# A running-maximum kernel: three engines' programs wrapped in a loop of two rounds, and Pool's products taken two rows at a time

## The chip, the cores and the metric

One core of one Trainium2 chip. The metric is the time of one execution on the device in microseconds, the median of several; a profile of one execution lies beside it. All runs told here were in the same, fast state. A ratio is the mean time of one kernel's fast runs over the mean time of the other's fast runs of the same rounds, so it isn't quite the ratio of the medians quoted. The experiments ran on three chips, each with the kernel before beside them.

## The reference

```python
# x: 8 x 2048 x 4096 float32 (268 MB), w: 4096 x 1
proj = (x @ w).squeeze(-1)                   # 8 x 2048 dot products of length 4096
cm = np.maximum.accumulate(proj, axis=1)
return np.cumsum((proj >= cm).astype(np.float32), axis=1)   # number of records so far
```

Every element of x is used once, so the time can't be below that of reading 268 MB.

## The kernel before

SyncE issues all loads of x. A tile is 128 partitions of 4 (later 3) rows of 4,096; three buffers of 8 MB take turns. Each row is split: VectorE makes the dot product of columns 0 to 2,815 in one instruction, Pool multiplies columns 2,816 to 4,095 and ACT sums that product. TensorE turns the sums so that VectorE can scan them. Eight tiles make a group; groups 0 to 2 are a loop on each engine, the rest is straight code.

```python
V, A, G, T, SY = nc.vector, nc.scalar, nc.gpsimd, nc.tensor, nc.sync
...
for g in range(NG):                        # NG = 4, rows per tile RS = (4, 4, 4, 3)
    r = RS[g]
    for t in range(B):                     # B = 8 tiles in a group, 3 buffers
        i = SY.dma_start(out=at(g, t)[:, : r * D], in_=x[B - 1 - t, ...]).then_inc(xs[t], 16)
        u, n = user_before(g, t)           # who had the buffer
        if n:
            i._wait_ge(*(free(u, n)))
        if g == t == 0:
            A.dma_start(out=w_row, in_=...).then_inc(ws, 16)
...
def group_products(r, g=0):                # Pool
    for t in range(B):
        for j in range(r):
            xl = at(g, t)[:, j * D + VC : (j + 1) * D]
            i = G.tensor_mul(out=xl, in0=xl, in1=w_sb).then_inc(pl, 1)
            if j == 0:
                i._wait_ge(xs[t], 16)

def group_sums(r, g=0):                    # ACT
    for t in range(B):
        for j in range(r):
            i = add_up(at(g, t)[...], sum_p[...])._wait_ge(pl, j + 1)
        i.then_inc(fr[t], 1)               # the buffer is free once VectorE and ACT have said so
        A.sem_inc(pl, -r)
    A.wait_ge(pd, 1).then_inc(pd, -1)

with A.Fori(0, NL):                        # NL = 3; VectorE, Pool and TensorE likewise
    group_sums(R)
group_sums(RS[-1], NL)
... # 128 more rows of each batch entry in ever smaller pieces, then the output
```

Of the kernel before, what the change touches and what calls it, by code (L numbers as in the profile page):

```python
# [2 lines left out]

os.environ.setdefault("NEURON_RT_ULTRASERVER_MODE", "4")

# [8 lines left out]
ACTF = mybir.ActivationFunctionType  # L15
NEG = -3.0e38
LOW = -3.2e38


@with_exitstack  # L20
def kernel(
# [15 lines left out]
    nc = tc.nc  # L37
    P = 128
    B, S, D = x.shape
# [3 lines left out]
    R = RS[0]  # L43
# [7 lines left out]
    VC = 2816  # L51
    PC = D - VC
# [15 lines left out]
    def rows_of(m):  # L68
        return m * H % B, m * H // B * Q
# [9 lines left out]
    def sb(shape, name, **kw):  # L79
        return pool.tile(shape, FP32, name=name, **kw)  # L80
# [6 lines left out]
    w_sb = sb([P, PC], "w_sb")  # L87
# [23 lines left out]
    def sem(name):  # L111
        return tc.alloc_semaphore(f"{name}_{next(ns)}")
# [3 lines left out]
    ws, bw, wc, cs, od, oe, psr, pd, pl, sd, pa, con, fo, ms, p7, mg, pg, ml = (  # L116
        sem(n) for n in "ws bw wc cs od oe psr pd pl sd pa con fo ms p7 mg pg ml".split()
    )
# [1 line left out]
    xq = [(ws, 32), (bw, NW + 16), (wc, 3 + 16), (con, 7 + 16), (fo, 1 + 16)]  # L120
    xq += [(s, 32) for s in xs[:5]] + [(s, 2 * NG + 16) for s in fr[:3]]

    V, A, G, T, SY = nc.vector, nc.scalar, nc.gpsimd, nc.tensor, nc.sync

    def dot(xsl, wsl, dst, seed=0.0):
        return V.tensor_tensor_reduce(  # L126
# [4 lines left out]
    def add_up(xsl, dst):  # L131
        return A.activation(out=xsl, in_=xsl, func=ACTF.Copy, accum_out=dst)  # L132
# [19 lines left out]
    def at(g, t):  # L152
        return xbuf[(t if g < NL else t + NS - 1) % NS]

    def user_before(g, t):
        if t >= NS:
            return t - NS, g + 1
        if g == NL:
            return B - NS + t, g
        return max(u for u in range(B) if u % NS == t), g  # L160

    def free(u, n):
        return (p7, n) if u == B - 1 else (fr[u], 2 * n)

    with tc.tile_critical(no_gpsimd_drain=True):

        for g in range(NG):
            r = RS[g]
            for t in range(B):
                i = SY.dma_start(  # L170
                    out=at(g, t)[:, : r * D],
                    in_=x[B - 1 - t, STARTS[g] : STARTS[g] + r * P, :].rearrange(
                        "(p r) d -> p (r d)", r=r
                    ),
                ).then_inc(xs[t], 16)
                u, n = user_before(g, t)
                if n:
                    i._wait_ge(*(free(u, n)))
                if g == t == 0:
                    A.dma_start(  # L180
                        out=w_row, in_=w.rearrange("(k c) one -> k (c one)", k=NW)
                    ).then_inc(ws, 16)
                if t == 4 and g:
                    SY.dma_start(
                        out=out[:, STARTS[g - 1] : STARTS[g]], in_=cnt
                    )._wait_ge(cs, g + 1).then_inc(od, 16)
# [9 lines left out]
        for i, (m, c0, c1, _, _) in enumerate(TILES):  # L196
            u, xb = slot(m)
            d = SY.dma_start(  # L198
                out=xb[:, c0:c1],
                in_=x[  # L200
                    rows_of(m)[0] : rows_of(m)[0] + H,
                    S0 + rows_of(m)[1] : S0 + rows_of(m)[1] + Q, c0:c1,
                ].rearrange("b i d -> i b d"),
            ).then_inc(xq[i][0], 16)
# [7 lines left out]
            out=identity, in_=identity, compare_op=ALU.not_equal, fill=1.0,  # L212
# [10 lines left out]
        for n, k in enumerate(order):  # L223
            c = k * WC
            dst = w_v[:, c : c + WC] if c < CV else ps
            i = T.matmul(  # L226
                out=dst, lhsT=identity[:NW, k : k + 1].to_broadcast([NW, P]),
                rhs=w_row, start=True, stop=True,
            ).then_inc(bw, 1)
# [11 lines left out]
            out=by_b, in_=identity.rearrange("p (i b) -> p b i", b=H),  # L241
# [3 lines left out]
            out=by_i, in_=identity.rearrange("p (i b) -> p i b", b=H), op=ALU.add,  # L245
            axis=mybir.AxisListType.X,
        ).then_inc(fo, 1)
        V.memset(ps[:B, :N], LOW)._wait_ge(wc, 3).then_inc(psr, 1)  # L248

# [4 lines left out]
        def group_dots(r, g=0):  # L254
            for t in range(B):
                b, xb = B - 1 - t, at(g, t)
                for j in range(r):
                    i = dot(
                        xb[:, j * D : j * D + VC], w_v[:, :VC],
                        sum_v[:, j * B + b : j * B + b + 1],  # L260
                    )
                    if j == 0:
                        i._wait_ge(xs[t], 16)
                i.then_inc(fr[t], 1)
# [6 lines left out]
        V.sem_inc(psr, -3)  # L271
        group_dots(RS[-1], NL)

        def group_products(r, g=0):
            for t in range(B):
                for j in range(r):
                    xl = at(g, t)[:, j * D + VC : (j + 1) * D]
                    i = G.tensor_mul(out=xl, in0=xl, in1=w_sb).then_inc(pl, 1)  # L278
                    if j == 0:
                        i._wait_ge(xs[t], 16)  # L280

        G.wait_ge(wc, 3)
        with G.Fori(0, NL):
            group_products(R)
            G.wait_ge(pg, 1).then_inc(pg, -1)
        group_products(RS[-1], NL)

        def group_sums(r, g=0):
            for t in range(B):
                b = B - 1 - t  # L290
                for j in range(r):
                    i = add_up(
                        at(g, t)[:, j * D + VC : (j + 1) * D],
                        sum_p[:, j * B + b : j * B + b + 1],
                    )._wait_ge(pl, j + 1)
                i.then_inc(fr[t], 1)
                A.sem_inc(pl, -r)
            A.wait_ge(pd, 1).then_inc(pd, -1)

        with A.Fori(0, NL):  # L300
            group_sums(R)
        group_sums(RS[-1], NL)

        def group_rows(r):
# [67 lines left out]
        for m in range(B - 2):  # L372
            k = m // 2
            v, p = acc_v[:, m : m + 1], acc_p[:, m : m + 1]
# [16 lines left out]
        for i in range(B - 2, len(TILES)):  # L391
            n = i - (B - 2)
            m, p = TILES[i][0], TILES[i][4]
# [21 lines left out]
        for a, b, n in ((STARTS[-1], S0, 1), (S0, S, 4)):  # L415
            SY.dma_start(
                out=out[:, a:b], in_=cnt[:, a - STARTS[-1] : b - STARTS[-1]]
            )._wait_ge(cs, NG + n).then_inc(oe, 16)
        G.wait_ge(oe, 32).then_inc(ml, 1)


# [28 lines left out]
```

## Time and profile before

| | before |
|---|---|
| time, median of 3 | 629.82 us (629.65 to 629.83) |
| busy: VectorE, Pool, ACT | 65%, 59%, 29% of the span |
| x read | 268.4 MB in 5,760 packets (queue q1 counts 6,560: 40 more of the output, 760 of 4 bytes) |
| the same, while the stream runs | 434.4 GB/s |
| instruction fetches in the span | 3 packets of 8 KB |

The prediction below shows the lines and reads them. A word on the views: the page lists the DMA queues by number (q1 carries x and the output, q10 the load of w, q14 instructions). In the timeline a row gives start, duration, engine, line of code, operation and, in brackets, the idle time before it and what ended it. The trace holds each DMA packet's start and duration as well; where the text speaks of packets, that is what it reads. A "straggler" is one of the 16 DMA engines whose packets of a tile end clearly after those of the others. The "spread" is the time from the first to the last of the 16 ends.

### The profile page before, as it was taken

How to read it: one execution, taken by the hardware profiler on the slowest of the kernel's cores; microseconds unless marked ns; L12 is line 12 of the kernel's file. 1: busy time of each engine (PE TensorE's matmuls, PEld its weight loads, DVE VectorE, ACT ScalarE, POOL GpSimd, SP SyncE). 2: the span in 40 equal slices, each digit the busy share in tenths (PEclk: the TensorE clock that was granted, in tenths of full speed). 3: DMA queues.
4: the chain of work that ended last, by engine and by line, in shares of the span. 5: the costliest groups of instructions: out<-in, count | busy, mean ns of one | idle time of the engine just before them, and what ended most of it. 6: DMA issues, size and time to landing. Idle time of an engine off the chain costs nothing. (4 is left out here: it accounts for less than half of the span.)

```text
span 627.8 us, 1141 instructions
## 1 busy us (share of the span) xinstructions
PE 29.4 (5%) x96; PEld 13.6 (2%) x96; DVE 407.2 (65%) x294; ACT 181.1 (29%) x274; POOL 370.5 (59%) x149
## 2 busy tenths in 40 slices
PE   8000000000020000000001000000002000000110
PEld 3000000000010000000000000000001000000000
DVE  0755676456776557755578655676556976655797
ACT  1222332123322233222233222332223333232244
POOL 0554676456765557745567555676557666655775
PEclk9999999999999999999996555555555555555565
DMA  9999999999999999999999999999999999999996
GB/s 402 401 468 401 468 401 464 406 463 405 463 405 463 405 463 405 465 405 463 405 463 405 463 405 459 409 460 409 459 420 423 436 442 420 443 442 410 430 429 261
DMA packets 6579, 268.55 MB, mean 428 GB/s; under 512 B 768, under 2 KB 1040, under 8 KB 1584
## 3 DMA queue, kind: packets, MB, share of 16 engines
q1 hardware_dynamic: 6560, 268.50, 98.9%
q14 instruction: 3, 0.02, 0.0%
q10 hardware_dynamic: 16, 0.02, 0.0%
HBM read 268.45 MB, written 0.07 MB: 428 GB/s over the span
## 5 line engine op out<-in xcount | busy, mean ns | idle before, releaser
L126 DVE CUSTOM_DVE_ANT_0 xall<-xall,w_v 128x2816 f32<-128x2816 f32 (+1 forms) x129 | 385.5, 3041 | 180.5 <-DMA xall<-in_x_dram 180.5
L278 POOL TENSOR_TENSOR xall<-xall,w_sb 128x1280 f32<-128x1280 f32 x120 | 344.8, 2905 | 245.9 <-DMA xall<-in_x_dram 242.6
L132 ACT ACTIVATE xall<-xall 128x1280 f32<-128x1280 f32 (+2 forms) x130 | 162.9, 1253 | 427.7 <-POOL xall L278 407.2
L314 PE MATMUL ps<-identity,small 128*8 128x128 f32 x60 | 13.4, 415 | 567.2 <-PEq L311 567.2
L132 ACT ACTIVATION_READ_ACCUMULATOR xall<-xall 128x1 f32 x130 | 24.2, 186 | 0.0
L338 POOL TENSOR_TENSOR xall<-xall,w_sb 128x1280 f32<-128x1280 f32 (+2 forms) x8 | 21.0, 2628 | 3.1 <-DMA xall<-in_x_dram 3.0
L314 PEld LDWEIGHTS ps<-identity,small 128*8 128x8 f32 x60 | 7.5, 128 | 574.3 <-issue 570.2
L142 DVE TENSOR_TENSOR_SCAN cm<-ps,cm,small 8x512 f32<-8x512 f32 (+3 forms) x8 | 7.0, 869 | 19.2 <-PE ps L314 18.8
L226 PE MATMUL w_v<-w,identity 8*128 8x512 f32 x14 | 12.2, 1056 | 0.0
L126 DVE DVE_READ_ACCUMULATOR2_ANT small<- 128x1 f32 x133 | 10.8, 81 | 0.0
L248 DVE MEMSET ps<- 8x512 f32 x1 | 0.5, 485 | 15.7 <-ACT w L237 15.7
L148 DVE TENSOR_TENSOR_SCAN cnt<-ps,cnt,small 8x512 f32<-8x512 f32 (+3 forms) x8 | 7.0, 871 | 0.3
L226 PEld LDWEIGHTS w_v<-w,identity 8*128 8x128 f32 x14 | 4.6, 332 | 7.3 <-issue 7.3
L234 ACT COPY w_sb<-w_v 128x768 f32<-128x768 f32 x1 | 0.8, 798 | 11.4 <-PE w_v L226 11.4
L145 DVE TENSOR_TENSOR ps<-ps,cm 8x512 f32<-8x512 f32 (+3 forms) x8 | 3.9, 486 | 0.3
L349 POOL TENSOR_TENSOR masked<-fold,small 128x4 f32<-128x4 f32 x8 | 1.6, 200 | 3.2 <-DVE small L126 3.2
L126 DVE CUSTOM_DVE_ANT_0 xall<-xall,w_v,small 128x480 f32<-128x480 f32 (+2 forms) x4 | 3.1, 810 | 0.2 <-DVE small L126 0.2
L359 PE MATMUL ps<-fold,masked 128*8 128x32 f32 x20 | 2.0, 234 | 25.3 <-ACT masked L354 17.7
L354 ACT ACTIVATE masked<-fold,small 128x4 f32<-128x4 f32 x10 | 3.0, 298 | 0.3
L338 POOL TENSOR_TENSOR xall<-xall,w 128x640 f32<-128x640 f32 (+1 forms) x2 | 2.3, 1136 | 0.1
L226 PE MATMUL ps<-w,identity 8*128 8x512 f32 x2 | 2.1, 1136 | 2.6 <-DMA w<-in_w_dram 2.6
L233 ACT ACT_TABLE_LOAD x1 | 1.3, 1283 | 2.7 <-DVE fold L244 2.7
(18 smaller groups left out, 5.3 us busy)
## 6 DMA issues: line engine op xcount, KB each, us to landing
xall<-in_x_dram SPq DMA_DIRECT2D x8, 6144.0 KB, 33.5
xall<-in_x_dram SPq DMA_DIRECT2D x6, 2048.0 KB, 42.6
xall<-in_x_dram SPq DMA_DIRECT2D x1, 1264.0 KB, 36.6
xall<-in_x_dram SPq DMA_DIRECT2D x1, 816.0 KB, 39.3
xall<-in_x_dram SPq DMA_DIRECT2D x1, 784.0 KB, 37.9
xall<-in_x_dram SPq DMA_DIRECT2D x2, 240.0 KB, 26.6
xall<-in_x_dram SPq DMA_DIRECT2D x1, 416.0 KB, 39.4
xall<-in_x_dram SPq DMA_DIRECT2D x24, 45.0
```

The costliest lines, as they stand in the source:

```text
L126: return V.tensor_tensor_reduce(out=xsl, in0=xsl, in1=wsl, scale=1.0, scalar=seed, op0=ALU.mult, op1=ALU.add, accum_out=dst,)
L132: return A.activation(out=xsl, in_=xsl, func=ACTF.Copy, accum_out=dst)
L142: V.tensor_tensor_scan(out=cm_, data0=src, data1=low, initial=cm0, op0=ALU.max, op1=ALU.max,)._wait_ge(psr, base).then_inc(psr, 1)
L145: V.tensor_tensor(out=src, in0=src, in1=cm_, op=ALU.is_ge)._wait_ge(psr, base + 1).then_inc(psr, 1)
L148: V.tensor_tensor_scan(out=cnt_, data0=src, data1=low, initial=cnt0, op0=ALU.add, op1=ALU.max,)._wait_ge(psr, base + 2).then_inc(cs, 1)
L226: i = T.matmul(out=dst, lhsT=identity[:NW, k : k + 1].to_broadcast([NW, P]), rhs=w_row, start=True, stop=True,).then_inc(bw, 1)
L278: i = G.tensor_mul(out=xl, in0=xl, in1=w_sb).then_inc(pl, 1)
L314: i = T.matmul(out=ps[:B, j : r * P : r], lhsT=l[:, j * B : (j + 1) * B], rhs=identity, start=k == 0, stop=k == 1,)
L338: G.tensor_mul(out=xl, in0=xl, in1=w_pool(*p))._wait_ge(*xq[i]).then_inc(pl, 1)
L349: return eng.tensor_tensor(out=e, in0=by_b, in1=acc.to_broadcast([P, H]), op=ALU.mult)
L354: return A.activation(out=e, in_=by_b, func=ACTF.Copy, scale=acc)._wait_ge(pa, na).then_inc(ms, 1)
L359: return T.matmul(out=ps[:B, k * Q : (k + 1) * Q], lhsT=masked[:, n * B : (n + 1) * B], rhs=by_i, start=start, stop=stop,)
```

## The change

Python objects record the three engines' programs and emit them later, inside `Fori(0, 2)` with an `If` on the counter. In round 0 the counter is zero, so each engine jumps over its whole program to its end and back again; round 1 runs it. The intent, as far as the code shows it: to touch the later blocks of the program at the very start, so that the instruction fetches don't fall into the stream of x. Besides, Pool takes two of four rows, or three of three, in one instruction, with w read through a zero stride.

```diff
-    V, A, G, T, SY = nc.vector, nc.scalar, nc.gpsimd, nc.tensor, nc.sync
+    V, A, G = Later(), Later(), Later()        # they record; issue() emits
+    T, SY = nc.tensor, nc.sync
...
-                    A.dma_start(
+                    nc.scalar.dma_start(
                         out=w_row, in_=...
...
+        w_one = w_sb.rearrange("p (o c) -> p o c", o=1)
+        def parts(r, t):
+            if r == R:
+                return [(0, R // 2), (R // 2, R)]
+            return [(j, j + 1) for j in range(r)] if t == B - 1 else [(0, r)]
...
-                for j in range(r):
-                    xl = at(g, t)[:, j * D + VC : (j + 1) * D]
-                    i = G.tensor_mul(out=xl, in0=xl, in1=w_sb).then_inc(pl, 1)
+                rows = at(g, t)[:, : r * D].rearrange("p (r d) -> p r d", r=r)
+                for j, k in parts(r, t):
+                    xl = rows[:, j:k, VC:]
+                    i = G.tensor_mul(
+                        out=xl, in0=xl, in1=w_one.to_broadcast([P, k - j, PC])
+                    ).then_inc(pl, 1)
...                                             # ACT waits at the first row of each part
+        for engine, program in ((nc.vector, V), (nc.scalar, A), (nc.gpsimd, G)):
+            with engine.Fori(0, 2) as i:
+                with engine.If(i):
+                    program.issue(engine)
```

More of the change, by code (lines that the diff above doesn't have):

```diff
@@ L2 @@
 import os
-from contextlib import ExitStack
+from contextlib import ExitStack, contextmanager
 os.environ.setdefault("NEURON_RT_ULTRASERVER_MODE", "4")
@@ L17, with __init__, __getattr__, note @@
 LOW = -3.2e38
+class Later:
+    def __init__(self):
+        self.todo = []
+    def __getattr__(self, name):
+        def note(*args, **kw):
+            step = Step(name, args, kw)
+            self.todo.append(step)
+            return step
+        return note
+    @contextmanager
+    def Fori(self, a, b):
+        outer, self.todo = self.todo, []
+        yield
+        outer.append((a, b, self.todo))
+        self.todo = outer
+    def issue(self, engine, todo=None):
+        for step in self.todo if todo is None else todo:
+            if isinstance(step, tuple):
+                a, b, inner = step
+                with engine.Fori(a, b):
+                    self.issue(engine, inner)
+            else:
+                step.issue(engine)
+class Step:
+    def __init__(self, name, args, kw):
+        self.calls = [(name, args, kw)]
+    def _wait_ge(self, *args):
+        self.calls.append(("_wait_ge", args, {}))
+        return self
+    def then_inc(self, *args):
+        self.calls.append(("then_inc", args, {}))
+        return self
+    def issue(self, engine):
+        for name, args, kw in self.calls:
+            engine = getattr(engine, name)(*args, **kw)
 @with_exitstack
@@ L290, in group_sums @@
                 b = B - 1 - t
+                begin = [j for j, _ in parts(r, t)]
                 for j in range(r):
@@ L294, in group_sums @@
                         sum_p[:, j * B + b : j * B + b + 1],
-                    )._wait_ge(pl, j + 1)
+                    )
+                    if j in begin:
+                        i._wait_ge(pl, begin.index(j) + 1)
                 i.then_inc(fr[t], 1)
-                A.sem_inc(pl, -r)
+                A.sem_inc(pl, -len(begin))
             A.wait_ge(pd, 1).then_inc(pd, -1)
@@ L418 @@
             )._wait_ge(cs, NG + n).then_inc(oe, 16)
-        G.wait_ge(oe, 32).then_inc(ml, 1)
+        for engine, program in ((nc.vector, V), (nc.scalar, A), (nc.gpsimd, G)):
+            with engine.Fori(0, 2) as i:
+                with engine.If(i):
+                    program.issue(engine)
+        nc.gpsimd.wait_ge(oe, 32).then_inc(ml, 1)
 _INS = ['x', 'w']
```

## The prediction

> **What bounds the kernel now.** I read the page first (shares, the 40 slices, the queues), then the chain that ended last, then the Pool timeline as a clock for landings, then the queue table cut into ever smaller windows, and at last the packets themselves.
>
> ```profile
> span 627.8 us, 1141 instructions
> PE 29.4 (5%) x96; PEld 13.6 (2%) x96; DVE 407.2 (65%) x294; ACT 181.1 (29%) x274; POOL 370.5 (59%) x149
> DMA  9999999999999999999999999999999999999996
> q1 hardware_dynamic: 6560, 268.50, 98.9%
> q14 instruction: 3, 0.02, 0.0%
> ```
>
> No compute engine is busy for more than two thirds, while the DMA engines are full in 39 of 40 slices. x alone is 268.4 MB. So the stream of x sets the time, and the rest is the start before it and the tail behind it. The chain that ended last says the same:
>
> ```profile
> 498.67 27.27 DMA xall<-in_x_dram
> 525.93 0.07 issue
> 526.00 8.64 POOL xall L278 x3
> ...
> 580.85 39.27 DMA xall<-in_x_dram
> 620.12 0.07 issue
> 620.19 1.76 POOL xall L338
> ```
>
> The reader should look at the two DMA pieces. A three-row tile occupies the stream for 14.5 us (the landings below), yet from issue to landing it takes 27.27 us: the load stood about 12.8 us in the queue behind others. The last one took 39.27 us for a few MB. So when an engine frees a buffer some microseconds earlier or later, only the queueing changes, not the landing. Behind the last landing lie 627.8 - 620.1 = 7.7 us: 5.3 us of sums, turns and scans, then the output's transfer and the closing barrier.
>
> The stream as seen by Pool, which starts on a tile as soon as it lands:
>
> ```profile
> 22.88 11.49 POOL L278 TENSOR_TENSOR xall<-xall,w_sb 128x1280 f32<-128x1280 f32 x4 [20.88 <-DMA xall<-in_x_dram]
> 42.17 11.48 POOL L278 TENSOR_TENSOR xall<-xall,w_sb 128x1280 f32<-128x1280 f32 x4 [7.80 <-DMA xall<-in_x_dram]
> 100.21 11.51 POOL L278 TENSOR_TENSOR xall<-xall,w_sb 128x1280 f32<-128x1280 f32 x4 [7.83 <-DMA xall<-in_x_dram]
> 120.22 11.49 POOL L278 TENSOR_TENSOR xall<-xall,w_sb 128x1280 f32<-128x1280 f32 x4 [8.50 <-DMA xall<-in_x_dram]
> 139.52 11.49 POOL L278 TENSOR_TENSOR xall<-xall,w_sb 128x1280 f32<-128x1280 f32 x4 [7.81 <-DMA xall<-in_x_dram]
> ```
>
> Tiles land every 19.30 us (139.52 - 120.22), except one: 120.22 - 100.21 = 20.01, which is 0.7 us more, and the idle time before it grows from 7.83 to 8.50. The lost time never comes back. The queue table of 95 to 125 us shows what is special there:
>
> ```profile
> q1 hardware_dynamic: 224, 12.58, 97.0%
> q14 instruction: 2, 0.02, 0.1%
> ```
>
> Two of the three instruction fetches of the whole run fall into that tile. Packet by packet: each of 16 DMA engines moves a 64 KB packet of x in 2.418 us, one straight after the other. At 104.362 and 116.460 us a fetch of 8,192 bytes takes 0.309 us on one of them and the x packet behind it takes 2.955 and 2.662 us, so those DMA engines fall 0.84 and 0.55 us behind. A tile has landed when the slowest has finished its eight packets. At the end of tile 4 the 16 ends span 0.50 us; at the end of tile 5 they span 1.07, with two stragglers (119.43 and 119.69 where the other fourteen lie in 118.62 to 119.13), and they stay stragglers, since no DMA engine ever idles. The third fetch, at 486.64, costs its DMA engine 0.53 us, but that one was early enough not to become the slowest.
>
> Who fetches? By 104 us VectorE had run 46 instructions, by 113.5 us ACT 55; at 486 us Pool had just left its loop, some 64 instructions into its program with the loop counted once. Three programs at a similar depth[...]. That these are VectorE, ACT and Pool is an inference, and they are the three that the change wraps.
>
> [...]
> [...]the back edges of the loops at about 171 and 326 us show no fetch at all.
> [...]the fetch at 104.362 starts where an x packet of its DMA engine ends (104.366), and the next x packet starts with the fetch's end.
> [...]One tile is 8.389 MB in 19.31 us = 434.4 GB/s[...].[...]
> [...]
>
> **The change part by part.**
> *The loop of two rounds.* Round 0 tests a register that is zero and branches over the whole program to its end; round 1 runs it. [...] Its effect, and I think its purpose, is that the jump enters the later blocks of code at about 1 us, before x saturates the DMA engines (first load issued at 0.97, first x packet at 2.00 us). The fetches then happen at the start and the stream runs undisturbed. If nothing remains at 104 and 116 us, the spread stays near 0.50 instead of 1.07, and every later landing, the last included, comes 1.07 - 0.50 = 0.57 us earlier. If the fetch still arrives just as the first x packets start, about 1 us after the branch, part of that is lost: an x packet waits up to 0.31 us on three DMA engines. But those are not necessarily the latest ones (the first x packets start anywhere from 2.00 to 2.53). I take 0.40 of the 0.57.
>
> *The later start of three engines.* Pool's identity matrix feeds the weights' broadcast on TensorE (2.6 to 16.6 us), ACT's copies (to 18.1) and VectorE's first scans (to 22.1); the first tile lands at 22.8. A start later by 0.5 us hides; one of 4 us[...] makes VectorE start on tile 0 some 3 us late. But VectorE needs 12.1 us of each 19.3 and Pool 11.5, and the first buffer is needed again only when tile 2 has landed near 61.5 us. Cost: 0. The load of w is issued ahead of the loop and isn't delayed.
>
> *Pool two rows at a time.* Durations by size: 2.905 us for 1,280 columns, 0.730 for 256, hence 2.12 ns per column and 0.19 us per instruction. Two rows: 2,560 x 2.12 + 190 = 5.62 us, where two took 5.74 back to back. A four-row tile: 11.2 instead of 11.5 us. Pool needs 30 fewer instructions of program (32 to 16 in the loop, 24 to 10 behind it). ACT gets its rows in pairs: its last sum ends about 11.2 + 2 x 1.4 = 14.0 us after landing instead of 12.9, and in a three-row tile (one instruction of three rows) 8.3 + 3 x 1.4 = 12.5 instead of 10.0. Buffers come free 1.1 to 2.5 us later against 12.8 us of queue ahead of the stream: 0 on the path. In each group's last three-row tile rows stay single, so the end of the group keeps its latency.
>
> *The tail.* The same instructions in the same order. The loop's exit (add, compare) comes after each engine's last instruction and under the output's transfer, 625.4 to 626.7: 0.
>
> Sum: -0.40 + 0 + 0 + 0, so 629.82 - 0.40 = 629.4 us.
>
> **The rivals.**
> (a) The fetches only move: the first round's fetches meet the first x packets and leave the same DMA engines as far behind as before; or the jump brings more fetches[...]. For it: the 1 us between a load's issue and its first packet is about the time a fetch needs too, so it is a close race. Against: at 2 us a fetch can still be ahead of the x packet. It would give 629.8, or with one more fetch on the slowest DMA engine 629.8 + 0.55 = 630.4.
> (b) A new wait: Pool's larger pieces, or the repeated reading of w through a zero stride, are slower than the durations say, so that buffers come late. Pool would have to go from 11.5 to over 19 us per tile, or a buffer to come 12 us later. Nothing in before speaks for a factor like that; even a rise by half would hide. If it did happen, 5% and more would be lost.
> (c) Nothing of it matters, since the tail is bound by compute: VectorE runs without idle time from 613.2 to 624.1 us. But it starts that run on a landing (0.89 us of waiting before it), so landings that all move by half a microsecond move it too. Otherwise 629.8.
>
> **Range and chances.** The point is the undisturbed stream at 70% of its 0.57. Below it lies the full gain and some scatter (three runs before differ by 0.18), so low 628.9; above it lies rival (a) with an extra fetch, so high 630.4. A change of 2% is 12.6 us. The whole time outside the stream is about 10 us, so faster by 2% can't be; slower would need rival (b). Faster 0.005, same 0.985, slower 0.01.
>
> **What would show each step.** In the profile after: the instruction queue has no packet between 10 and 620 us, but some at the start; Pool's tile 5 comes 19.3 and not 20.0 us behind tile 4; landings from tile 5 on come about half a microsecond earlier, and the last near 619.6; the chain still ends through the last DMA landing; a Pool instruction of 128x2560 takes about 5.6 us, one of 128x3840 about 8.3; Pool waits for each tile's landing as before; ACT waits longer for its first rows. The prediction is wrong if fetches still lie in the stream, if the first tile lands later than 22.8 by as much as the stream gains, if a two-row product takes over 8 us, or if the tail behind the last landing becomes longer than 7.7 us.

The sum stands as it was put, -0.40 + 0 + 0 + 0, so 629.82 - 0.40 = 629.4 us: no term of it is cut. The 0.5 us of later start that "hides" is only an assumption, and that a jump brings the fetches forward was conjecture, which the profile of before didn't show. Nor did it show how long a fetch takes to come, "about the time" of a load; x_late measured that later, 1.1 us from jump to packet.

## The result

| | before | after |
|---|---|---|
| time, median | 629.83 us (629.65 to 629.84, 4 runs) | 629.92 us (629.83 to 630.01, 4 runs) |
| ratio after / before | | 1.0002, interval 0.9985 to 1.0019 |
| span of the profiled run | 627.8 | 627.9 |
| instruction fetches at | 104.4, 116.5, 486.6 us | 5.2, 5.3, 7.6 us |
| first x packet | 2.00 | 2.00 |
| tile 0: end of the slowest DMA engine, spread | 22.46, 0.48 | 23.02, 1.05 |
| tile 5: the same | 119.69, 1.07 | 119.61, 0.78 |
| tile 23: the same | 467.60, 1.07 | 467.65, 0.67 |
| last packet of x | 622.81 | 622.85 |

The page of the changed kernel, the lines that answer to those of before:

```profile
span 627.9 us, 1106 instructions
PE 29.3 (5%) x96; PEld 13.8 (2%) x96; DVE 407.2 (65%) x294; ACT 174.3 (28%) x274; POOL 361.5 (58%) x87
DMA  9999999999999999999999999999999999999996
q14 instruction: 3, 0.02, 0.0%
```

Pool ran 62 instructions fewer in 9 us less. The three fetches are still there. The queue table of the changed kernel's first 10 us shows where:

```profile
q1 hardware_dynamic: 49, 3.21, 82.2%
q10 hardware_dynamic: 16, 0.02, 1.1%
q14 instruction: 3, 0.02, 0.6%
```

The same table from 95 to 125 us, where before had two fetches, now has x alone:

```profile
q1 hardware_dynamic: 227, 12.78, 98.6%
```

And Pool's timeline as the clock of the landings:

```profile
23.53 11.20 POOL L65 TENSOR_TENSOR xall<-xall,w_sb 128x2560 f32<-128x2560 f32 x2 [20.49 <-DMA xall<-in_x_dram]
42.83 11.21 POOL L65 TENSOR_TENSOR xall<-xall,w_sb 128x2560 f32<-128x2560 f32 x2 [8.10 <-DMA xall<-in_x_dram]
100.74 11.20 POOL L65 TENSOR_TENSOR xall<-xall,w_sb 128x2560 f32<-128x2560 f32 x2 [8.10 <-DMA xall<-in_x_dram]
120.07 11.21 POOL L65 TENSOR_TENSOR xall<-xall,w_sb 128x2560 f32<-128x2560 f32 x2 [8.12 <-DMA xall<-in_x_dram]
139.36 11.20 POOL L65 TENSOR_TENSOR xall<-xall,w_sb 128x2560 f32<-128x2560 f32 x2 [8.08 <-DMA xall<-in_x_dram]
```

Read it against the five rows of before. The step at tile 5 is gone (120.07 - 100.74 = 19.33; it was 20.01), but tile 0 lands at 23.53 where it landed at 22.88: 0.65 us later. From tile 5 on the two clocks agree within 0.2 us (save at the first three-row tile, at 483.84 and 482.79, where Pool did not wait for a landing). So the loss was moved from tile 5 to tile 0. The chain that ended last comes through the same load at the same time as before (620.12 there):

```profile
583.10 37.04 DMA xall<-in_x_dram
620.14 0.07 issue
620.21 1.76 POOL xall L65
```

The packets say why. VectorE and Pool jump at 1.14 and 1.06 us, ACT at 1.68 (it issues the load of w first, 0.60 us). Three fetches follow on three DMA engines, at 5.219 and 5.280 us behind x's first packet and at 7.646 us behind its second, and leave those engines 0.84 to 0.55 us behind: the x packets after them take 2.949, 2.942 and 2.659 us in place of 2.418. These are the costs of 104 and 116 us again. No engine waited for these fetches: Pool ran the end of its program at 1.52 us, 0.45 us after its jump, VectorE at 1.74 and ACT at 2.17, before any of the three had run. So none of the three brought the code at the target; what they brought, the runs don't show.

### The profile page after: what moved, and what is told of

Same layout as the page of the kernel before. It is cut to its first block, busy times and chain, and to the rows that moved or that the text cites. A ratio compares the mean times of both kernels' runs of the same rounds, so it can differ in the third digit from the quotient of the medians.

```text
span 627.9 us, 1106 instructions
## 1 busy us (share of the span) xinstructions
PE 29.3 (5%) x96; PEld 13.8 (2%) x96; DVE 407.2 (65%) x294; ACT 174.3 (28%) x274; POOL 361.5 (58%) x87
## 5 line engine op out<-in xcount | busy, mean ns | idle before, releaser
L65 POOL TENSOR_TENSOR xall<-xall,w_sb 128x2560 f32<-128x2560 f32 (+3 forms) x66 | 356.8, 5426 | 257.0 <-DMA xall<-in_x_dram 252.3
L376 PE MATMUL ps<-identity,small 128*8 128x128 f32 x60 | 13.3, 415 | 567.3 <-PEq L373 567.3
```

The costliest lines, as they stand in the source:

```text
L65: engine = getattr(engine, name)(*args, **kw)
L376: i = T.matmul(out=ps[:B, j : r * P : r], lhsT=l[:, j * B : (j + 1) * B], rhs=identity, start=k == 0, stop=k == 1,)
```

## The experiments

Two questions were open. First, do stragglers made by instruction fetches really set the time, and would it fall by the 0.57 us of the prediction if the fetches were out of the way? Rivals: all 16 DMA engines share one limit, so that a straggler means nothing; or Pool's larger pieces cost what the fetches gained. Second, is the later freeing of buffers free of charge?

Means over all runs of a kernel, with the mean of the kernel before in the same rounds:

| run | mean us (runs) | before us | first x packet | last x packet after the first | fetches at |
|---|---|---|---|---|---|
| rows_only | 629.89 (4) | 629.80 | 1.99 | 620.94 | 104, 117, 593 |
| loop_only | 630.18 (4) | 629.80 | 1.99 | 620.80 | 5.3, 5.3, 7.5 |
| x_late | 631.91 (4) | 629.80 | 4.09 | 620.93 | 2.1, 2.3, 2.8 |
| x_late_again | 631.67 (5) | 629.94 | 4.09 | 620.49 | 2.1, 2.3, 2.8 |
| before_late | 631.91 (5) | 629.94 | 4.16 | 621.14 | 107, 119, 489 |
| early | 630.06 (5) | 629.94 | 2.40 | 620.41 | 2.1, 2.1, 2.3 |
| early3 | 630.35 (5) | 629.97 | 2.24 | 621.35 | 2.1, 2.1, 5.8 |
| pad256 | 631.49 (4) | 629.80 | 1.99 | 622.51 | 7.6, 13.3, 106, 119, 489 |
| pad512 | 634.69 (4) | 629.97 | 2.01 | 625.72 | 7.8, 13.5, 19.3, 25.1, 108, 121, 492 |
| rows_four | 631.83 (4) | 629.97 | 2.01 | 622.30 | 5.1, 7.5, 7.6 |
| no_compute | 629.19 (4) | 629.97 | 2.00 | 620.87 | 104, 107, 476 |

The fifth column is from the one profiled run of each: last packet's end minus first packet's start. It is 620.81 for before and 620.85 for after. It takes out the different starts.

**rows_only: Pool's part alone.**

```diff
         for engine, program in ((nc.vector, V), (nc.scalar, A), (nc.gpsimd, G)):
-            with engine.Fori(0, 2) as i:
-                with engine.If(i):
-                    program.issue(engine)
+            program.issue(engine)
```

> Only Pool's two and three rows per instruction, no loop of two rounds. Theory (the slowest of the 16 DMA engines sets the landings, and a fetch of instructions behind which x packets wait makes it slowest): VectorE's and ACT's fetches stay in the stream at about 104 and 116 us, Pool's moves later or goes; spread of the DMA engines' ends at tile 5 about 1.07 us as before; time 629.8, within 0.3. Rival (Pool's larger pieces and later frees cost something of their own, which the loop would have to make good): over 630.2.

629.89 against 629.80 us: no difference that the times could show, as expected; by profile x took 620.94 us from first to last packet, against 620.81. Two fetches stay at 104.5 and 116.6 us and give the spread of 0.94 at tile 5. The third came at 592.8 instead of 486.6, so it was Pool's, whose program had become shorter. The rival, that the pairs of rows cost half a microsecond, has no support, though the times alone couldn't exclude it.

**loop_only: the loop alone.**

```diff
         def parts(r, t):
-            if r == R:
-                return [(0, R // 2), (R // 2, R)]
-            return [(j, j + 1) for j in range(r)] if t == B - 1 else [(0, r)]
+            return [(j, j + 1) for j in range(r)]
```

> Only the loop of two rounds, Pool one row at a time. Theory: three fetches at 5 to 8 us as in the changed kernel, tile 0 lands about 0.6 us later than before and tile 5 at the same time as before; time 629.9, within 0.3. Rival (the pairs of rows cost the half microsecond that the moved fetches gained): about 629.4.

630.18 against 629.80 us, ratio 1.0006 (0.9990 to 1.0023): at the edge of what was expected, and not distinguishable from no change. Fetches at 5.25, 5.33 and 7.50 us; the last x packet ends 620.80 after the first, as in before. By these profiles (620.94 and 620.80 against 620.81) neither half of the change moved the stream by half a microsecond: it isn't plus half and minus half.

**x_late: let the fetches go first, at a price.** In this and the next the first load waits for Pool's preparing instructions.

```diff
+        SY.wait_ge(con, 7)
         for g in range(NG):        # the loads of x
```

> The changed kernel, with the first load of x held until Pool's seven preparing instructions are done, near 3.0 us instead of 0.97, so that the fetches have idle DMA engines. Theory: the fetches' packets run before x's first (at about 4 us), the ends of the DMA engines at tile 0 span about 0.5 us with no stragglers, and the time is 629.9 + 2.1 - 0.57 = 631.4. Rival (stragglers don't set the time, for instance because all 16 share one limit): 629.9 + 2.1 = 632.0 with the same spread of landings relative to the start. Third possibility: the fetches come later than 4 us even on idle DMA engines; then the spread stays near 1 us and the time is 632.0 too.

The fetches ran at 2.14, 2.32 and 2.78 us on idle DMA engines. So they need 1.1 us from jump to packet (VectorE and Pool jump at 1.15 and 1.07 us, ACT at 1.68). A load's first packet in the changed kernel starts at 2.00: the race was lost by 0.1 to 0.8 us. The spread at tile 0 was 0.49 us without stragglers. But the time was 631.91, which is the rival's figure. The profile shows what came in between. From 24 to 93 us all sixteen DMA engines lost time, in packets up to 0.2 us longer than 2.418, some 15 us in sum or 0.9 us each. Such stretches are called bouts below, and the time by which the 64 KB packets exceed 2.418 us, summed over all of them, the excess. Neither theory had this. So the control and a repetition:

**before_late and x_late_again.** The first is the kernel before, with its first load held for as long.

```diff
+        late = sem("late")
+        SY.wait_ge(con, 7)
+        for _ in range(18):
+            SY.sem_inc(late, 1)
         for g in range(NG):        # the loads of x
```

> Control for the run with the late load: the kernel before, its fetches left in the stream, with the first load of x held by the same two microseconds or so (a wait for Pool's seven instructions and a row of dummy increments). If stragglers alone set the time, this is 629.85 plus the hold, near 631.9, and lies 0.5 us above the late-load run at the same first packet. If the bulk of the DMA engines loses about as much by itself as the stragglers lost, the two are equal within 0.2 us.

> The late-load run once more, the very same kernel, for more times and a second profile. Its first profile had no stragglers (spread 0.49 us at tile 0) and yet all 16 DMA engines lost about 0.9 us each between 24 and 93 us. If that was chance, this profile doesn't show it and the time is near 631.4; if the DMA engines disturb each other when they run in step, it shows it again (over 10 us of excess over all 64 KB packets) and the time stays near 631.9.

The queue table of the repetition for 0 to 4 us shows the fetches with no x beside them:

```profile
q14 instruction: 3, 0.02, 2.0%
q10 hardware_dynamic: 16, 0.02, 1.8%
```

and from 4 to 628 us no fetch:

```profile
q1 hardware_dynamic: 6550, 268.50, 99.6%
```

631.67 with the fetches out of the way, 631.91 with them in the stream, on the same chip; the control started 0.07 us later, which leaves 0.17 us. The first x_late run had shown none. By profile, x took 620.49 us in the repetition and 621.14 in the control. The bouts came again: the excess was 7.9 us in the repetition and 8.6 in the control, in patches between 33 and 114 us, in the repetition with packets up to 0.27 us too long. So neither of the two forecasts of the repetition came true: the excess was under 10 us, and the time lay between 631.4 and 631.9.

| profile | stragglers from fetches | median DMA engine's end of tile 23, after the first packet | slowest one's |
|---|---|---|---|
| before | yes | 464.70 | 465.61 |
| loop_only | yes | 464.67 | 465.60 |
| after | yes | 465.12 | 465.65 |
| before_late | yes | 465.10 | 465.94 |
| early | no | 465.01 | 465.29 |
| x_late_again | no | 465.13 | 465.38 |
| x_late | no | 465.53 | 465.82 |

This table is the answer to the first question as far as it goes. The slowest DMA engine of a tile sets the landing (in before the slowest ended tile 5 at 119.69 us, the median one at 118.91, and Pool began at 120.22). With stragglers present, the median engine may lose up to half a microsecond to bouts without any effect, because the stragglers are still later (after: median 0.42 us later than before, slowest the same). Without stragglers such a loss shows at once. The gain from clean fetches is therefore not the 0.57 us by which the stragglers stood out. In these profiles it was 0.2 to 0.65 us against before and control, and nothing for x_late; in the times it is below the noise.

**early: no hold beyond what the race needs.** ACT jumps before it loads w, and SyncE runs six dummy increments ahead of its first load.

```diff
+        late = sem("late")
+        for _ in range(6):
+            SY.sem_inc(late, 1)
         for g in range(NG):        # the loads of x
...
-                    nc.scalar.dma_start(
+                    A.dma_start(
                         out=w_row, in_=...
```

> The changed kernel with the load of w moved behind ACT's loop top, so that ACT jumps 0.6 us sooner, and six dummy increments ahead of the first load of x (about 0.4 us), so that the fetches, which reach the DMA engines 1.1 us after the jump (2.14 and 2.32 us in the late-load run), come just ahead of x's first packets. Theory: fetches at 2.0 to 2.4 us, no stragglers, spread at tile 0 about 0.5 us, time 629.85 + 0.4 - 0.57 = 629.7. If the bulk's own loss takes the place of the stragglers': 630.2.

The fetches won: 2.12, 2.13, 2.32 us, x at 2.40. The spread was 0.70 at tile 0 and fell to 0.40 by tile 23, and x took 620.41 us, the shortest of all profiles, 0.40 less than in before. The hold had cost 0.40. Time 630.06 against 629.94: nothing left. The mean lies nearer the second figure that was expected (630.2, the bulk's own loss takes the stragglers' place) than the first (629.7).

**early3: half the hold.**

```diff
-        for _ in range(6):
+        for _ in range(3):
```

> The run with the early fetches, with three dummy increments in place of six: x's first packet near 2.2 instead of 2.4 us. Fetches at 2.12, 2.13 and 2.32 us then meet x's first packets, which start over half a microsecond. Theory: one or none of the three falls behind an x packet; spread at tile 0 0.5 to 0.9 us; time 629.7, between 629.5 and 630.0. If the fetches lose the race again they come at 5 to 8 us and the time is 630.1.

630.35 us, worse than expected. Two fetches ran at 2.13; the third lost and ran at 5.84:

```profile
q1 hardware_dynamic: 22, 1.44, 112.0%
q10 hardware_dynamic: 4, 0.01, 0.7%
q14 instruction: 1, 0.01, 0.6%
```

(the queue table of 5 to 8 us; a packet counts whole where it starts, hence a share over 100%). That one was enough: its DMA engine ended tile 0 at 23.69 where the next-latest ended at 22.83, and it stayed last by 0.95 us at tile 23. There is no version here that beats both kernels.

**pad256: more fetches.** 256 one-column fills at the head of VectorE's program, in its idle time.

```diff
+        for n in range(256):
+            V.memset(dead[:, n : n + 1], 0.0)
         V.tensor_reduce(out=by_b, ...)
```

> The kernel before with 256 one-column fills put at the head of VectorE's program, in time in which VectorE would wait anyway (2 to 18 us); its program is 256 instructions longer, so two more fetches of 8 KB come into the stream. Theory: each puts the DMA engine that serves VectorE's fetches another 0.55 to 0.85 us behind the other fifteen; with all three on the same one the landings and the time come 1.1 to 1.4 us later: 630.9 to 631.3. Rival (a fetch costs its DMA engine time, but stragglers don't set the time): 629.8.

631.49 against 629.80 us, +1.69, somewhat over the expected 1.1 to 1.4. In the packets one DMA engine ends tile 0 at 23.92, 1.30 us behind the next. Pool begins tile 0 at 24.45 us (22.88 in before, +1.57) and tile 5 at 121.93 (120.22, +1.71), and the last x packet comes 1.70 us later than in before. At tile 23 the slowest DMA engine is 1.70 us later than in before (469.30), the median one 0.25 us (466.95). So a straggler does set the time, microsecond for microsecond, once it stands out beyond the rest. The rival of a shared limit is out. VectorE's timeline (from 2 us on) shows the block size and the stall, too:

```profile
1.97 0.79 DVE L242 MEMSET dead<- 128x1 f32 x27
3.15 3.63 DVE L242 MEMSET dead<- 128x1 f32 x128 [0.39 <-issue]
9.37 1.92 DVE L242 MEMSET dead<- 128x1 f32 x67 [2.58 <-issue]
```

The first row holds the last 27 of 60 fills that began at 1.03 us. The engine halts after these 60 and again after exactly 128 more: in this run a block is 128 instructions (256 fills brought two more fetches, each a packet of 8,192 bytes, so 64 bytes per instruction). The second halt lasts 2.58 us, from 6.78 to 9.37; the fetch, which had to wait behind an x packet, ran within it, at 7.62 to 7.93 us.

**pad512: a second dose.** The same edit with 512.

> A second dose: 512 fills at the head of VectorE's program in place of 256, two more fetches of 8 KB. With 256 the DMA engine that serves VectorE's fetches was 1.9 us behind its neighbours and the time 1.6 us longer. Theory: in proportion, another 1.1 to 1.7 us: 632.6 to 633.2. VectorE starts on tile 0 some 15 to 20 us late, which alone is hidden by the three buffers. Rival (the time doesn't follow the slowest DMA engine): 631.5 as with 256.

634.69 us, above the expected 632.6 to 633.2. Most of it is the dose, which was larger than put. Pool's timeline begins tile 1 at 45.90 us, 3.73 later than in before, where with 256 it was 1.58 later (43.75): 2.15 us for two more fetches. Each takes 0.32 us, and the x packet behind it 3.08 in place of 2.418, which makes 0.98 us; two of these and a little more. The rest came later. By the last three-row tile (589.02 us, 584.10 in before) the delay had grown to 4.92 us. At 158 us the trace shows how: a tile counts as landed only with its last DMA engine, so the one straggler, almost 4 us behind, delayed the freeing of buffers, and the load for the next group was issued at 156.3 us, when the other fifteen had little over a microsecond of queue left. At 158.0 us only nine of the sixteen had a packet of x under way. So a straggler that was almost 4 us behind starved others.

**rows_four: are later frees free?**

```diff
-            if r == R:
-                return [(0, R // 2), (R // 2, R)]
+            if r == R and t < B - 1:
+                return [(0, R)]
```

> The changed kernel with four rows in one Pool instruction for all but the last tile of a group: ACT can begin only 11.1 us after a landing and the buffer comes free near 16.2 us after it instead of 14.4. The claim is that frees have over 10 us to spare, so the time is 629.9 within 0.3 and the gaps between landings stay 19.3 us. Rival (frees matter): the loads come later by 1.8 us per tile that waits, and the time is above 631.

The claim fell: 631.83 against 629.97 us, ratio 1.0032 (1.0017 to 1.0048). The claim of 12.8 us to spare had been read in the last, three-row group. At the start of a group the margin is another. The load of tile 0 of the next group waits for tile 6 of the one before, and by then only tile 7 is queued. It is issued at 152.4 us in before, 153.2 in after, 155.9 with four rows; the first DMA engine runs out of x at 157.3, 157.5 and 158.1. Less the 1.03 us from issue to packet, the margin is 3.9 us in before, 3.3 in after and 1.1 with four rows, and 1.05 at the next group (issue 310.6, first end 312.7). There, at 313.2, the first x packet on one DMA engine took 0.41 us too long. At tile 20 one DMA engine ended 0.47 us behind the next, where none had stood out at tile 15.

```profile
294.40 11.05 POOL L65 TENSOR_TENSOR xall<-xall,w_sb 128x5120 f32<-128x5120 f32 x1 [8.27 <-DMA xall<-in_x_dram]
313.74 11.49 POOL L65 TENSOR_TENSOR xall<-xall,w_sb 128x1280 f32<-128x1280 f32 x4 [8.29 <-DMA xall<-in_x_dram]
333.34 11.04 POOL L65 TENSOR_TENSOR xall<-xall,w_sb 128x5120 f32<-128x5120 f32 x1 [8.11 <-DMA xall<-in_x_dram]
```

333.34 - 313.74 = 19.60, 0.3 us over the usual step. That isn't the whole 1.8 us. Against after, this profile lost 0.47 us in a bout at 118 to 139 us and 0.66 us among the last, small pieces of x; what these two have to do with four rows, the runs don't show.

**no_compute: where do the bouts come from?** All products and sums of x cut to 8 columns; the results are wrong.

```diff
-            out=xsl, in0=xsl, in1=wsl, scale=1.0, scalar=seed,
+            out=xsl[:, :8], in0=xsl[:, :8], in1=wsl[:, :8], scale=1.0, scalar=seed,
...                                 # ACT's sums and Pool's products likewise
```

> The kernel before with every product and sum of x cut to 8 columns: wrong results on purpose, the same loads, waits and instructions. It asks whether the bouts in which all DMA engines lose time (excess over 2.418 us per 64 KB packet) come from the engines' own traffic to the on-chip memory. If so: no bouts, excess of about 1.5 us in all, which is the fetches' alone. If they come from the loads themselves or from outside: bouts as in the other profiles, 3 us or more of excess in all. The last load lands near 622.8 either way, since the fetches' stragglers stay; the time is 2 to 3 us shorter by the shorter work behind the last landing: about 627.

```profile
PE 29.4 (5%) x96; PEld 13.7 (2%) x96; DVE 34.0 (5%) x294; ACT 35.8 (6%) x274; POOL 25.2 (4%) x149
```

With VectorE, Pool and ACT nearly idle (4 to 6% busy) there were still bouts, between 31 and 90 us: 3.9 us of excess in all, of which 0.8 are the x packets behind fetches. So the engines' traffic to the on-chip memory isn't needed for them. Their cause stays open; across the profiles the whole excess ranged from 1.6 us (loop_only) to 15.1 (x_late), the first two packets of each DMA engine left out, and pad512 too, whose DMA engines starved (39 us). The last x packet ended 620.87 us after the first (620.81 in before), as expected. The forecast of 627 us missed: cutting nearly all the work on x saved 0.8 us, which the interval of the ratio (0.9974 to 1.0005) doesn't even tell from nothing.

## Why the prediction was right or wrong

It said 629.4 us, 628.9 to 630.4, and "same" with 0.985. Measured: 629.92, ratio 1.0002. The range and the class hold, but that is no merit of the mechanism: the range took in rival (a), and a gain of 0.40 us lies within the ±1 us of the times. By the packets the gain did not come; rival (a), "The fetches only move", did, almost word for word, and with it the prediction's own sign of being wrong, a first tile that lands later by as much as the stream gains (0.65 us).

- *What bounds the kernel: right.* x's stream sets the end in both kernels. Two added fetches cost 1.69 us (pad256), and cutting nearly all compute on x moved the mean by 0.8 only, which also speaks against rival (c), a tail bound by compute.
- *A fetch in the stream makes a straggler that stays: right* (0.53 to 0.84 us each in before, 0.98 in pad512), and it holds for fetches at 5 us as for those at 104. Who fetches was an inference. The change moved all three fetches; rows_only moved the third alone, as Pool's would.
- *The loop brings the fetches ahead of x: the step that failed.* In the prediction's words: "I take 0.40 of the 0.57." It saw a close race and took 70% of the gain. The race was lost three times out of three: 1.1 us from jump to packet (measured in x_late), so 2.14 us at the earliest, against x's first packet at 2.00, and ACT's jump delayed by its load of w. The forecast of part of an overlap ("an x packet waits up to 0.31 us") was wrong in kind: in the changed kernel no fetch shared the time with x's first packet; each stood behind an x packet, and then cost the full 0.55 to 0.84 us.
- *0.57 us as what clean fetches are worth: too large.* Where they did come first, x's stream was 0.40 us (early) and 0.32 us (x_late_again) shorter than in before by profile, and 0.12 us longer in x_late. The prediction had compared the stragglers with the other DMA engines of one profile, as if the others were always as undisturbed as there.
- *The expected signs:* the first two came true without any gain: no fetch after 10 us, and tile 5 at 19.33 us behind tile 4. The third failed: landings from tile 5 on weren't half a microsecond earlier, and the one looked for near 619.6 came at 620.14.
- *Misread, without effect on the sum:* 620.12 is the landing on the chain, not the last one. Later loads land until 623.16 us, and the last x packet ends at 622.81, so that only some 5 of the 7.7 us lie behind the stream. The load of 39.27 us carries 816 KB and not "a few MB".
- *Pool's durations: right.* 5.62 us predicted for two rows, 5.63 measured; 8.3 for three, 8.32 measured. The last sum of tile 0 ends 13.9 us after the landing (14.0 predicted).
- *Buffers freed later cost 0: right for this change, with a wrong reason.* rows_only shows no cost beyond the noise. But the margin at a group's start is some 4 us in before, not 12.8, and rows_four, which frees 3.5 us later than before, was 1.9 us slower, of which the narrow margin explains a part.
- *The start: no cost, right, but longer than the 0.5 us reckoned with.* Pool's round 0 took from 0.93 to 2.0 us, about 1 us. Round 0's compare-and-branch has a record of 0.05 to 0.07 us, but the next instruction began 0.45 us (Pool) to 0.59 us (VectorE) after its start, and the jump back took 0.25 to 0.29 us from start to start. VectorE's first scans ended at 22.2 us and still came before the first landing.

## What to carry to other kernels

In this kernel, which keeps all DMA engines full from start to end, a foreign packet stayed in the time where it made its DMA engine the slowest (pad256: the slowest one 1.70 us later at tile 23, the median one 0.25, the time 1.69); look for the slowest of the sixteen, not for the mean. The early fetches left no straggler only where they ran before the stream (early: 2.12 to 2.32 us, x at 2.40; after: x at 2.00, the fetches at 5.2 to 7.6). So compare the latency of both before paying for it (here 1.1 us from jump to fetch, 1.03 us from the issue of a load to its first packet), and count what a delay of the stream costs (early won the race and still gained nothing that the times show: 630.06 against 629.94). And read the margin of a buffer at its tightest place (here the first load of each group, 3.9 us in before), not where the chain of waits happens to pass (12.8 us).
